# A seven-product FFN pair accumulated in two PSUM banks, and gated products turned by transposing DMAs

## The chip, the cores and the metric

The kernel runs on one core of one Trainium2 chip. The metric is device time in microseconds (us) of one execution; several executions of one build are timed and their median is taken. Beside them stands one execution that was recorded by the hardware profiler, with a span (first to last instruction) and a time of its own.

The engines of the core are named as in the profile: PE is TensorE's matmul (PEld its weight load), DVE is VectorE, ACT is ScalarE, POOL is GpSimd, SP is SyncE, on whose queue this kernel puts its DMAs.

## What is computed

Two layers of an encoder trunk over 256 tokens of width 1024. Each layer is a projection, two attention-like branches, their merge, a SwiGLU feed-forward network (FFN) and an embedding step. The change lies in the FFN:

```python
gate, up = jnp.split(rms_norm(h, g_ffn_pre) @ w_ffn_in, 2, axis=-1)     # (256,1024) @ (1024, 2*2816)
h = h + rms_norm((jax.nn.silu(gate) * up) @ w_ffn_out, g_ffn_post)       # (256,2816) @ (2816,1024)
```

## The kernel before

**Split products.** Every float32 operand is kept as two parts, a rounded high part and the remainder. `split` (L112) makes them: an ACT cast gives the high part, a DVE subtraction (through `vsub`, L108) the low part. A product of two split operands is three matmuls (`mm3`, whose matmuls carry L96). A weight unit is 512 x 512; its splitting is two ACT casts and two DVE subtractions of 128 x 1024.

**The weight stream.** `Stream` loads units over SP into two `raw` buffers (or into borrowed ones, "lent" and "big", for the pairs below), splits them up to four ahead of PE, and issues the next load (L259) when a raw buffer comes free. `ws.take()` hands a unit to PE, `ws.done()` frees it and lets the next unit be split.

**The FFN.** The hidden width 2816 is eleven blocks of 256. For each block the gate and up columns are multiplied with the normed activations of the two token halves (`hf` 0 and 1); silu(gate) times up is the *gated product* of 128 tokens x 256 hidden channels per half. To be multiplied by `w_ffn_out` it has to be turned, so that hidden channels lie on partitions, and split; `hid` holds the turned parts.

- Blocks 0 and 1 come first, each half by itself (silu on L1257), then *plain* blocks 4, 5 and 10 (`block`, silu on L1274): one unit serves both halves with 24 matmuls.
- Blocks 2-3, 6-7 and 8-9 are three *pairs* (`pair`, `seven`). The four 128x512 results of a pair (gate and up of two halves) are a 2x2 block product, and they are formed from seven unit products instead of eight, at the price of sums of activations (`sums`, once per layer) and sums of weight units (`Stream.step`: four DVE sums of 128x2048 per pair, L289 to L300). A product (`times`, matmuls on L568 or, with the plain activations, also L568) is 12 matmuls.
- In `seven`, before the change, five of the seven products went to PSUM banks of their own or were added to; three were copied out by ACT (L612, L617, L624), and five DVE sums of 128x512 put them together: `vsub(v, o, p1)`, three additions through `add` (L607), and `vsub(v, p5, c22)` ahead of the second half's silu (L1297).

**Turning.** There are two ways in the kernel. `transpose_in` (L427) and the copy of it in `block` (L1282) use PE: transposes against an identity into a PSUM bank, then `split` reads PSUM. All gated products were turned so. `Split.turn_words` is used elsewhere, for the branch outputs ("gg") and for half of the merge: ACT copies the 32-bit words apart into their two 16-bit halves (L404), a transposing DMA on SP's queue turns them (L410), ACT copies the halves together again (L414), and `split` reads SBUF.

**The order of the work.** A string fixes the order of the FFN for PE; `u` is half a plain block (one unit), a digit is a product of a pair, `o` is one unit of `w_ffn_out` for both halves (`out_step`), `p` loads what the later stages need:

```python
FFN = "uu12u34u5u67" "uo12o34o5o67" "poo12o345o67"
PLAIN, PAIRS = (4, 5, 10), (2, 6, 8)
```

Delayed work is a `Task`, a generator that yields the number of *ticks* to wait; `tick()` is called after every six matmuls or so on PE, and a task that is due puts its instructions at that place of the program. PE's turning waited 4 ticks (`WAIT_FFN`) after a block, 9 (`WAIT_PAIR`) after a pair, 3 and 4 (`WAIT_LAST`) after the last pair. `turn_words` waits 3 ticks (`SENT`) between the first ACT copy and the DMA, and 9 (`LANDED`) between the DMA and the second copy. A consumer that comes sooner forces the task (`need`). A scheduler then orders each engine's instructions by priority and modelled readiness; each engine executes its own list in order. `tc.high_priority(n)` moves instructions forward in it.

**Buffers.** PSUM has eight banks (`acc`, `aux`). The 512-wide SBUF tiles `t512` (names `t_...` in the profile) have seven buffers; a turning by words takes three of them beside the gated product.

Of the kernel before, what the change touches and what calls it, by code (L numbers as in the profile page):

```python
# [15 lines left out]
ALU = mybir.AluOpType  # L16
# [10 lines left out]

WAIT, WAIT_FIRST, WAIT_NEXT, WAIT_H, WAIT_FFN, WAIT_MIX = 6, 4, 9, 5, 4, 3
W = dict(r=5, z=6, s0=4, s=3, s1=9, o0=1, o=1, k=4, q=3, a0=1, a1=4, a2=4, a3=1, g=6)
# [11 lines left out]

WAIT_PAIR, WAIT_LAST = 9, (3, 4)
SENT, LANDED, NEXT = 3, 9, 2
# [7 lines left out]
def trunk_kernel(ctx: ExitStack, tc: tile.TileContext, a: dict, out: bass.AP):  # L51
# [158 lines left out]
    class Stream:  # L210
# [74 lines left out]
        def step(self, n, x, y, z, q):  # L285
            c = slice(0, 2048)
            if n == 1:
                self.made(x)
                nc.vector.tensor_tensor(out=x.raw[:, c], in0=x.raw[:, c], in1=z.raw[:, c], op=ALU.add)  # L289
            elif n == 2:  # L290
                self.made(y)
                nc.vector.tensor_tensor(out=z.raw[:, c], in0=z.raw[:, c], in1=y.raw[:, c], op=ALU.add)
            elif n == 3:
                self.made(x)
                nc.vector.tensor_tensor(out=x.raw[:, c], in0=x.raw[:, c], in1=y.raw[:, c], op=ALU.add)
            elif n == 4:
                self.made(z)
            elif n == 5:
                self.made(x)
                nc.vector.tensor_tensor(out=x.raw[:, c], in0=x.raw[:, c], in1=q.raw[:, c], op=ALU.add)  # L300
            elif n == 6:
                self.made(q)
            else:
                self.load()
                self.made(x)
                self.held -= 1
                self.lend = True
# [55 lines left out]
    class Split:  # L363
# [29 lines left out]

        def turn_words(self, src, k, n, hf):

            x = lambda: t512()[:, : n * P]
            w = x()
            w16 = w.bitcast(U16)
            nc.scalar.copy(  # L404
                w16.rearrange("p (s c) -> p s c", s=2), src.bitcast(U16).rearrange("p (c s) -> p s c", s=2)
            )
            yield SENT
            r = x()
            r16 = r.bitcast(U16)
            nc.sync.dma_start_transpose(out=r16.rearrange("p (r t) -> p r t", t=P), in_=w16)  # L410
            yield LANDED
            z = x()
            z16 = z.bitcast(U16)
            nc.scalar.copy(z16.rearrange("p (c s) -> p s c", s=2), r16.rearrange("p (s c) -> p s c", s=2))  # L414
            self.put(z, k, n, hf * P, P)

# [158 lines left out]
    def sums(x):  # L575
# [7 lines left out]
        def make():  # L583
# [16 lines left out]
    def seven(sp, forms, gated):  # L600
# [4 lines left out]

        def add(out, x, y):
            nc.vector.tensor_tensor(out=out, in0=x, in1=y, op=ALU.add)  # L607
# [4 lines left out]
        nc.scalar.copy(p1, c11)  # L612
# [24 lines left out]
        times(p5, quad(1, 1), False)  # L637
        vsub(v, p5, c22)
        gated(1, v, c22)
        yield  # L640
# [164 lines left out]
    for l in range(DEPTH):  # L805
# [457 lines left out]
        def block(b):  # L1263
            sg = t512()
            o = [acc(), acc()]
            for kh in range(2):
# [4 lines left out]
                if kh == 1:  # L1271
# [4 lines left out]

                    def turn():
                        yield WAIT_FFN
                        ps = aux()
                        for k in range(2):  # L1280
                            for hf in range(2):
                                nc.tensor.transpose(  # L1282
                                    ps[:, k * T + hf * P : k * T + (hf + 1) * P],
                                    sg[:, hf * 256 + k * P : hf * 256 + (k + 1) * P], ident,
                                )
                        with tc.high_priority(AHEAD):
                            hid.put(ps, 2 * b, 2, 0, T)

                    t = Task(turn(), part[0], 2 * b // 4)
                    for hf in range(2):  # L1290
# [3 lines left out]
        def pair(b):  # L1294
            def gated(hf, gate, up):
                sg = t512()
                nc.scalar.activation(sg, gate, AF.Silu)  # L1297
# [163 lines left out]
```

## Time and profile before

| what | us |
|---|---|
| median of 3 runs | 933.05 (932.12 to 935.67) |
| the profiled execution, its own time | 931.35 |
| the span of that execution, first to last instruction | 929.6 |
| first FFN matmul to the first matmul of the embedding step, layer 0 | 256.34 to 437.87 |
| the same stage of layer 1, end | 893.82 |

The mean granted TensorE clock of the profiled execution is 0.998. PE is busy for 99% of the span, DVE for 79%, ACT for 63%. A busy time is the time in which at least one instruction is under way on the engine; matmuls overlap in the pipeline, so that what a matmul costs is read from the distance between the starts of two, not from its own duration. A wait in the profile is idle time of one engine in front of an instruction, with the instruction that ended it.

### The profile page before, as it was taken

The numbers are of one execution on the slowest core, as the hardware profiler recorded it, in microseconds if no ns is written. First come the engines' busy times: TensorE is split into PE (matmuls) and PEld (weight loads), VectorE is DVE, ScalarE is ACT, GpSimd is POOL, SyncE is SP. The second block draws the span as 40 slices with busy tenths as digits, with TensorE's granted clock in tenths as the row PEclk, the third lists the DMA queues.
The fourth block names the chain that finished last, engine by engine and source line by source line (L and its number), as shares of the span: only waits on it lengthen the run. The fifth ranks groups of instructions, "written<-read, shape, count | busy, mean of one in ns | idle before, by whom it ended". The sixth has DMA issues, their size and how long they took to land.

```text
span 929.6 us, 12279 instructions
## 1 busy us (share of the span) xinstructions
PE 916.4 (99%) x4649; PEld 777.9 (84%) x4649; DVE 732.8 (79%) x933; ACT 587.4 (63%) x952; POOL 82.3 (9%) x150
## 2 busy tenths in 40 slices
PE   8999999999999999999999999999999999999996
PEld 7998888888878888888899988888888788888886
DVE  4798977556569999998789799665666798989974
ACT  5669678735467565566766686785546656656663
POOL 3500211000000000002023001200001000000000
PEclk9999999999999999999999999999999999999999
DMA  7464457767385565537555525396662937473551
GB/s 246 155 227 135 138 180 183 243 214 208 98 270 167 187 228 210 185 142 249 195 168 182 192 81 180 103 294 200 205 218 94 309 121 271 150 264 118 182 181 45
DMA packets 100760, 172.39 MB, mean 185 GB/s; under 512 B 16023, under 2 KB 39063, under 8 KB 100702
## 3 DMA queue, kind: packets, MB, share of 16 engines
q1 hardware_dynamic: 100702, 171.62, 55.8%
q8 instruction: 36, 0.59, 0.3%
q14 instruction: 22, 0.18, 0.1%
HBM read 167.41 MB, written 1.05 MB: 181 GB/s over the span
## 4 chain that ended last, share of the span: by engine, by line
PE 81%; DVE 9%; DMA 3%; ACT 2%; issue 2%; POOL 1%; SPq 0%; POOLq 0%; ACTq 0%; DVEq 0%
PE acc_0ffnin L96 11%; PE acc_1ffnin L96 7%; PE acc_0ffnin L568 6%; PE acc_0gate L96 5%; PE acc_1gate L96 5%; PE acc_1merge L96 5%; PE acc_0merge L96 5%; DVE wl_1ffnin L108 4%; PE acc_1ffnin L568 3%; PE acc_1gqk L96 2%; PE acc_0gqk L96 2%; PE acc_1ple L96 2%; PE acc_0rq L96 2%; PE acc_0gg L96 2%; PE acc_1gg L96 2%; PE acc_0v L96 2%
## 5 line engine op out<-in xcount | busy, mean ns | idle before, releaser
L96 PE MATMUL acc_1ffnin<-wh_1ffnin,big_1ffnin 128*128 128x512 f32 x176 | 56.9, 393 | 0.0
L96 PE MATMUL acc_0ffnin<-wh_0ffnin,big_0ffnin 128*128 128x512 f32 x176 | 56.9, 392 | 0.0
L112 ACT CAST wh_1ffnin<-raw_1ffnin 128x1024 fp32r<-128x1024 f32 x38 | 38.0, 1049 | 22.5 <-PE acc_1ffnin L96 7.6
L112 ACT CAST wh_0ffnin<-raw_0ffnin 128x1024 fp32r<-128x1024 f32 x38 | 37.9, 1050 | 21.0 <-PE acc_0ffnin L96 7.7
L108 DVE TENSOR_TENSOR wl_1ffnin<-raw_1ffnin,wh_1ffnin 128x1024 fp32r<-128x1024 f32 x38 | 44.8, 1219 | 4.4 <-ACT wh_1ffnin L112 4.2
L108 DVE TENSOR_TENSOR wl_0ffnin<-raw_0ffnin,wh_0ffnin 128x1024 fp32r<-128x1024 f32 x38 | 45.3, 1232 | 3.4 <-ACT wh_0ffnin L112 3.2
L96 PEld LDWEIGHTS acc_1ffnin<-wh_1ffnin,big_1ffnin 128*128 128x128 f32 x176 | 33.0, 188 | 7.0 <-ACT big_1ffnin L112 0.4
L96 PEld LDWEIGHTS acc_0ffnin<-wh_0ffnin,big_0ffnin 128*128 128x128 f32 x176 | 33.0, 188 | 6.7
L108 DVE TENSOR_TENSOR wl_1ffnin<-lent_1ffnin,wh_1ffnin 128x1024 fp32r<-128x1024 f32 x30 | 35.4, 1218 | 2.0 <-ACT wh_1ffnin L112 1.9
L108 DVE TENSOR_TENSOR wl_0ffnin<-lent_0ffnin,wh_0ffnin 128x1024 fp32r<-128x1024 f32 x30 | 35.5, 1219 | 1.8 <-ACT wh_0ffnin L112 1.7
L112 ACT CAST wh_1ffnin<-lent_1ffnin 128x1024 fp32r<-128x1024 f32 x30 | 30.2, 1050 | 8.6 <-ACT wh_1ffnin L112 3.0
L112 ACT CAST wh_0ffnin<-lent_0ffnin 128x1024 fp32r<-128x1024 f32 x30 | 30.2, 1050 | 8.6 <-PE acc_0ffnin L96 3.7
L96 PE MATMUL acc_1ffnin<-wl_1ffnin,big_1ffnin 128*128 128x512 f32 x88 | 34.3, 390 | 0.0
L96 PE MATMUL acc_0ffnin<-wl_0ffnin,big_0ffnin 128*128 128x512 f32 x88 | 34.3, 389 | 0.0
L96 PE MATMUL acc_0ffnin<-wh_0ffnin,big_0wout 128*128 128x512 f32 x96 | 31.2, 395 | 0.0
L96 PE MATMUL acc_1ffnin<-wh_1ffnin,big_1wout 128*128 128x512 f32 x96 | 31.2, 394 | 0.0
L568 PE MATMUL acc_0ffnin<-wh_0ffnin,mid_0ffnin 128*128 128x512 f32 x96 | 31.0, 390 | 0.0
L568 PE MATMUL acc_1ffnin<-wh_1ffnin,mid_1ffnin 128*128 128x512 f32 x96 | 31.0, 390 | 0.0
L108 DVE TENSOR_TENSOR wl_0gate<-raw_0gate,wh_0gate 128x1024 fp32r<-128x1024 f32 x14 | 16.5, 1221 | 15.2 <-ACT wh_0gate L112 15.2
L108 DVE TENSOR_TENSOR wl_1gate<-raw_1gate,wh_1gate 128x1024 fp32r<-128x1024 f32 x14 | 16.5, 1222 | 15.2 <-ACT wh_1gate L112 15.2
L96 PE MATMUL acc_0rq<-wh_start,big_start 128*128 128x384 f32 (+1 forms) x96 | 24.8, 343 | 1.0 <-ACT big_start L122 1.0
L96 PE MATMUL acc_1gate<-wh_1gate,big_0ple 128*128 128x512 f32 x80 | 24.8, 389 | 0.0
(655 smaller groups left out, 2948.9 us busy)
## 6 DMA issues: line engine op xcount, KB each, us to landing
raw_0ffnin<-in_w_ffn_out_dram SPq DMA_DIRECT2D x11, 1024.0 KB, 5.7
raw_1ffnin<-in_w_ffn_out_dram SPq DMA_DIRECT2D x11, 1024.0 KB, 5.0
lent_0ffnin<-in_w_ffn_in_dram SPq DMA_DIRECT2D x6, 1024.0 KB, 7.4
lent_1ffnin<-in_w_ffn_in_dram SPq DMA_DIRECT2D x6, 1024.0 KB, 7.5
raw_0rq<-in_w_in_dram SPq DMA_DIRECT2D x4, 1024.0 KB, 5.1
raw_0v<-in_w_in_dram SPq DMA_DIRECT2D x4, 1024.0 KB, 5.1
raw_0gg<-in_w_in_dram SPq DMA_DIRECT2D x4, 1024.0 KB, 5.1
raw_0gate<-in_w_o_gla_dram SPq DMA_DIRECT2D x4, 1024.0 KB, 5.1
```

What stands on the lines that cost most here:

```text
L96: return nc.tensor.matmul(o, lhsT, rhs, start=start, stop=stop)
L108: nc.vector.tensor_tensor(out=out, in0=in0, in1=in1, op=ALU.subtract)
L112: nc.scalar.copy(hi, src)
L568: nc.tensor.matmul(o, x, y, start=first and k + n == 0, stop=k == 3 and n == 2, skip_group_check=not first)
```

## The change

1. `seven` uses two PSUM banks, `a` and `v`, for products 1 to 5 and 7, and a third, `c`, for product 6. Products 3, 5 and 7 are added into `a` on top of the first, product 4 into `v` on top of the second (the matmuls run with `start` off, once what is in the bank has been read). ACT still copies out three times. Of the DVE sums, three are left: `vsub(u, v, u)`, `vsub(p5, p5, a)` and an addition `p1 = c + p1`, the last two with raised priority. The first half's silu reads SBUF (`p1`) and the second half's reads PSUM (`a`).
2. `sums` forms its sums with other signs and another order of the four; their number stays. `Stream.step` sums the weight units in another order (x+z, x+y, z+y, x+q) and makes them in the order x, x, x, y, z, q, x, where it was x, y, x, z, x, q, x.
3. All gated products but the last pair's go through `turn_words`. Per layer these are four of 128x256 (blocks 0 and 1), three of 128x512 that hold both halves of a plain block, and four of 128x512 (two pairs): 11 transposing DMAs. The last pair keeps `transpose_in` and its 3 and 4 ticks.
4. `turn_words` gets a form for both halves at once, whose second ACT copy is two copies of half the size.

```diff
         def step(self, n, x, y, z, q):
...
+            if n == 7:
+                self.load()
+            self.made((x, x, x, y, z, q, x)[n - 1])
             if n == 1:
-                self.made(x)
-                nc.vector.tensor_tensor(out=x.raw[:, c], in0=x.raw[:, c], in1=z.raw[:, c], op=ALU.add)
+                add(x, z)
             elif n == 2:
-                self.made(y)
-                nc.vector.tensor_tensor(out=z.raw[:, c], in0=z.raw[:, c], in1=y.raw[:, c], op=ALU.add)
-            elif n == 3:
-                self.made(x)
-                nc.vector.tensor_tensor(out=x.raw[:, c], in0=x.raw[:, c], in1=y.raw[:, c], op=ALU.add)
+                add(x, y)
             elif n == 4:
-                self.made(z)
+                add(z, y)
             elif n == 5:
-                self.made(x)
-                nc.vector.tensor_tensor(out=x.raw[:, c], in0=x.raw[:, c], in1=q.raw[:, c], op=ALU.add)
-            elif n == 6:
-                self.made(q)
...
+                add(x, q)
...
-        def turn_words(self, src, k, n, hf):
+        def turn_words(self, src, k, n, hf=None):
-            x = lambda: t512()[:, : n * P]
+            x = lambda: t512()[:, : n * P * (2 if hf is None else 1)]
...
-            nc.scalar.copy(z16.rearrange("p (c s) -> p s c", s=2), r16.rearrange("p (s c) -> p s c", s=2))
-            self.put(z, k, n, hf * P, P)
+            if hf is None:
+                for i in range(2):
+                    nc.scalar.copy(
+                        z16.rearrange("p (k h t s) -> p h s k t", k=2, h=2, s=2)[:, i],
+                        r16.rearrange("p (s h k t) -> p h s k t", h=2, k=2, s=2)[:, i],
+                    )
+                self.put(z, k, n, 0, T)
+            else:
+                nc.scalar.copy(z16.rearrange("p (c s) -> p s c", s=2), r16.rearrange("p (s c) -> p s c", s=2))
+                self.put(z, k, n, hf * P, P)
...
         def make():
             yield 1
             (a11, a12), (a21, a22) = x
             s2 = t512()
             vsub(a22, a21, a22)
-            vsub(s2, a11, a22)
-            vsub(a12, a12, s2)
+            vsub(s2, a22, a11)
+            nc.vector.tensor_tensor(out=a12, in0=a12, in1=s2, op=ALU.add)
             yield 1
-            vsub(a21, a21, a11)
-            for s in (a12, a22, a21, s2):
+            vsub(a21, a11, a21)
+            for s in (a22, s2, a12, a21):
...
-        (p1, v), (p3, p7) = (halves(mid()) for _ in range(2))
-        c11 = acc()
-        times(c11, quad(0, 0))
-        nc.scalar.copy(p1, c11)
+        (p1, p5), u = halves(mid()), mid()[:, 0:512]
+        a, v = acc(), acc()
+        times(a, quad(0, 0))
+        nc.scalar.copy(p1, a)
         yield
         task.need()
-        o = acc()
-        times(o, form(0))
-        nc.scalar.copy(p3, o)
+        times(v, form(0))
+        nc.scalar.copy(p5, v)
         yield
-        p5 = acc()
-        times(p5, form(1))
+        times(a, form(1), False)
+        nc.scalar.copy(u, a)
         yield
-        o = acc()
-        times(o, form(2))
-        nc.scalar.copy(p7, o)
+        times(v, form(2), False)
+        vsub(u, v, u)
         yield
-        o = acc()
-        times(o, form(3))
-        vsub(v, o, p1)
-        add(v, p5, v)
-        c12, c22 = p3, p7
-        add(c12, v, p3)
-        add(c22, v, p7)
+        times(a, form(3), False)
+        with tc.high_priority(EMPTY):
+            vsub(p5, p5, a)
         yield
-        times(c11, quad(0, 1), False)
-        gated(0, c11, c12)
+        c = acc()
+        times(c, quad(0, 1))
+        with tc.high_priority(EMPTY):
+            nc.vector.tensor_tensor(out=p1, in0=c, in1=p1, op=ALU.add)
+            gated(0, p1, u)
         yield
-        times(p5, quad(1, 1), False)
-        vsub(v, p5, c22)
-        gated(1, v, c22)
+        times(a, quad(1, 1), False)
+        gated(1, a, p5)
         yield
...
-        def turned(src, k, n, hf, wait=WAIT_FFN):
+        def turned(src, k, n, hf, wait=None):
             def turn():
-                yield wait
-                transpose_in(hid, src, k, n, hf)
+                if wait in WAIT_LAST:
+                    yield wait
+                    transpose_in(hid, src, k, n, hf)
+                else:
+                    yield from hid.turn_words(src, k, n, hf)
...
-                    def turn():
-                        yield WAIT_FFN
-                        ps = aux()
-                        for k in range(2):
-                            for hf in range(2):
-                                nc.tensor.transpose(
...
-                    t = Task(turn(), part[0], 2 * b // 4)
+                    t = Task(hid.turn_words(sg, 2 * b, 2), part[0], 2 * b // 4)
...
-                turned(sg, 2 * b, 4, hf, WAIT_LAST[hf] if b == PAIRS[-1] else WAIT_PAIR)
+                turned(sg, 2 * b, 4, hf, WAIT_LAST[hf] if b == PAIRS[-1] else None)
```

More of the change, by code (lines that the diff above doesn't have):

```diff
@@ L26 @@
 AHEAD, EMPTY, EMPTY_FIRST = 400, 100, 1600
-WAIT, WAIT_FIRST, WAIT_NEXT, WAIT_H, WAIT_FFN, WAIT_MIX = 6, 4, 9, 5, 4, 3
+WAIT, WAIT_FIRST, WAIT_NEXT, WAIT_H, WAIT_MIX = 6, 4, 9, 5, 3
 W = dict(r=5, z=6, s0=4, s=3, s1=9, o0=1, o=1, k=4, q=3, a0=1, a1=4, a2=4, a3=1, g=6)
@@ L40 @@
 OUT = (0, 1, 2, 3, 4, 5, 10, 6, 7, 8, 9)
-WAIT_PAIR, WAIT_LAST = 9, (3, 4)
+WAIT_LAST = (3, 4)
 SENT, LANDED, NEXT = 3, 9, 2
@@ L285, in step, with add @@
         def step(self, n, x, y, z, q):
-            c = slice(0, 2048)
+            def add(to, other):
+                c = slice(0, 2048)
+                nc.vector.tensor_tensor(out=to.raw[:, c], in0=to.raw[:, c], in1=other.raw[:, c], op=ALU.add)
+            if n == 7:
+                self.load()
+            self.made((x, x, x, y, z, q, x)[n - 1])
             if n == 1:
-                self.made(x)
-                nc.vector.tensor_tensor(out=x.raw[:, c], in0=x.raw[:, c], in1=z.raw[:, c], op=ALU.add)
+                add(x, z)
             elif n == 2:
-                self.made(y)
-                nc.vector.tensor_tensor(out=z.raw[:, c], in0=z.raw[:, c], in1=y.raw[:, c], op=ALU.add)
-            elif n == 3:
-                self.made(x)
-                nc.vector.tensor_tensor(out=x.raw[:, c], in0=x.raw[:, c], in1=y.raw[:, c], op=ALU.add)
+                add(x, y)
             elif n == 4:
-                self.made(z)
+                add(z, y)
             elif n == 5:
-                self.made(x)
-                nc.vector.tensor_tensor(out=x.raw[:, c], in0=x.raw[:, c], in1=q.raw[:, c], op=ALU.add)
-            elif n == 6:
-                self.made(q)
-            else:
-                self.load()
-                self.made(x)
+                add(x, q)
+            elif n == 7:
                 self.held -= 1
@@ L1275, in block @@
                         vmul(sg[:, c], o[hf][:, 256:512], sg[:, c])
-                    def turn():
-                        yield WAIT_FFN
-                        ps = aux()
-                        for k in range(2):
-                            for hf in range(2):
[L1282 to L1287, printed above, removed]
-                    t = Task(turn(), part[0], 2 * b // 4)
+                    t = Task(hid.turn_words(sg, 2 * b, 2), part[0], 2 * b // 4)
                     for hf in range(2):
```

2 lines of the change are left out of this document (removed).

## Prediction

> **What bounds the kernel now.** I read the page first: busy times, then the chain of work that ended last.
>
> ```profile
> span 929.6 us, 12279 instructions
> PE 916.4 (99%) x4649; PEld 777.9 (84%) x4649; DVE 732.8 (79%) x933; ACT 587.4 (63%) x952; POOL 82.3 (9%) x150
> PE 81%; DVE 9%; DMA 3%; ACT 2%; issue 2%; POOL 1%; SPq 0%; POOLq 0%; ACTq 0%; DVEq 0%
> ```
>
> PE holds 81% of the chain, DVE 9%. The share of the whole span hides the stages, so the windows over layer 0's FFN came next (columns: window, its length, then busy us and count of PE, PEld, DVE, ACT, POOL, clock, DMA share, GB/s):
>
> ```profile
> 266.00:300.00 34.00, 33.66 (x155) 27.27 (x155) 29.06 (x36) 22.04 (x34) 0.00 (x0) 1.00 0.64 211
> 300.00:340.00 40.00, 39.92 (x181) 32.78 (x180) 37.15 (x36) 22.89 (x30) 0.00 (x0) 1.00 0.72 260
> 340.00:390.00 50.00, 50.00 (x228) 41.31 (x227) 45.85 (x42) 29.68 (x35) 0.95 (x1) 1.00 0.51 184
> 390.00:437.80 47.80, 47.80 (x224) 39.61 (x223) 43.68 (x43) 31.29 (x40) 5.65 (x12) 1.00 0.51 178
> ```
>
> PE idles 0.42 us in 171.8 (the four lengths less the four busy times), so each instruction taken out of PE's stream should shorten the stage. But DVE is busy for 93% of 300 to 340, 92% of 340 to 390 and 91% from 390 on. It follows close behind, and ACT, at 105.9 us of 171.8 (62%), feeds it. The question is whether DVE and ACT can follow a faster PE.
>
> **PE: the transposes that go.** The turnings of layer 0, by line, and one group of four in the timeline:
>
> ```profile
> L1282 PE MATMUL aux_0ffnin<-ident,t_0ffnin x12: 270/272/329, 298.3 to 343.9; 128*128 128x128 f32 x12
> L427 PE MATMUL aux_0ffnin<-ident,t_0ffnin x32: 270/272/275, 269.8 to 425.6; 128*128 128x128 f32 x32
> ```
>
> ```profile
> 338.82 0.39 PE L96 MATMUL acc_0ffnin<-wh_0ffnin,big_0ffnin 128*128 128x512 f32 x1
> 339.05 0.60 PE L427 MATMUL aux_0ffnin<-ident,t_0ffnin 128*128 128x128 f32 x4
> 339.40 0.47 PE L96 MATMUL acc_0ffnin<-wh_0ffnin,big_0ffnin 128*128 128x512 f32 x1
> 339.72 0.39 PE L96 MATMUL acc_0ffnin<-wl_0ffnin,big_0ffnin 128*128 128x512 f32 x1
> ```
>
> The duration of 272 ns is latency; the cost is the shift of the starts. From 338.82 the second matmul after the group starts 0.90 later; two matmul steps take 0.46 (two steps of 0.23, as from 338.82 to 339.05). So four transposes cost 0.44, one 0.11. Of 44 per layer the last pair keeps 8; 36 go: 36 x 0.11 = 4.0 us per layer, **8.0 us in both**. PE's other work stays: seven products, as before.
>
> **DVE: the sums that go.** The rows of the additions in `seven`:
>
> ```profile
> L607 DVE TENSOR_TENSOR mid_0ffnin<-mid_0ffnin,mid_0ffnin x6: 681/688/693, 326.6 to 415.3; 128x512 f32<-128x512 f32 x6
> L607 DVE TENSOR_TENSOR mid_0ffnin<-acc_0ffnin,mid_0ffnin x3: 683/685/692, 325.9 to 413.9; 128x512 f32<-128x512 f32 x3
> ```
>
> Two sums less per pair, three pairs: 6 x 0.69 = 4.1 us of DVE per layer. With PE idle 0.42 us, I count no gain on the path; they buy slack, and only from the end of the first pair on (325.9). The splits of the turned parts stay, from SBUF in place of PSUM; the weight sums stay four of 128x2048. `sums` keeps four sums.
>
> **ACT, SP and DMA: what is added.** Turning by words can be priced where the kernel does it already (the "gg" tiles: the two ACT copies, the cast, the DMA's issue):
>
> ```profile
> L404 ACT COPY t_0gg<-mid_0gg x4: 1034/1042/1058, 142.0 to 156.2; 128x1024 uint16<-128x1024 uint16 x4
> L410 SPq DMA_TRANSPOSE t_0gg<-t_0gg x4: 1237/1294/5613, 143.1 to 158.9; - x4
> L414 ACT COPY t_0gg<-t_0gg x4: 1348/1358/1364, 159.8 to 170.1; 128x1024 uint16<-128x1024 uint16 x4
> DMA to landing us min/median/max: 3.1/5.1/7.7
> ```
>
> (The last line is from the view of L410.) A 512-wide turning adds 1.04 + 1.36 = 2.4 us of ACT, a 256-wide one half, by estimate: 7 x 2.4 + 4 x 1.2 = 21.6 us per layer. ACT goes from 105.9 to about 127.5 of 168, 76%: not a bound by its sum. The DMA waits 3 ticks and has 9 ticks to land; a tick is six matmuls, 6 x 0.23 = 1.4 us, so 12 us against a landing of at most 7.7. By the string, blocks 4, 5, 10 and pairs 2 and 6 are turned 8 ticks or more before `out_step` asks; no task is forced. What can hurt is order: ACT executes its list in order, and the first copy stands behind the DVE product it reads, the second behind the landing. The merge shows both (ACT's timeline, the bracket being the idle time):
>
> ```profile
> 210.27 1.05 ACT L404 COPY t_0merge<-big_0gate 128x1024 uint16<-128x1024 uint16 x1 [2.80 <-DVE big_0gate L1213]
> 215.38 1.35 ACT L414 COPY t_0merge<-t_0merge 128x1024 uint16<-128x1024 uint16 x1 [1.22 <-DMA t_0merge<-t_0merge]
> ```
>
> Queued behind such a copy are the casts of the next weight units; DVE waits for these, then PE. The tight place is the first pair, where DVE and PE run side by side:
>
> ```profile
> 276.76 1.22 DVE L108 TENSOR_TENSOR wl_0ffnin<-raw_0wout,wh_0ffnin 128x1024 fp32r<-128x1024 f32 x1 [4.26 <-ACT wh_0ffnin L112]
> 287.91 2.28 DVE L289 TENSOR_TENSOR lent_0ffnin<-lent_0ffnin,lent_0ffnin 128x2048 f32<-128x2048 f32 x1
> 295.52 2.35 DVE L108 TENSOR_TENSOR wl_0ffnin<-raw_0ffnin,wh_0ffnin 128x1024 fp32r<-128x1024 f32 x2
> 298.45 2.35 DVE L108 TENSOR_TENSOR wl_0ffnin<-lent_0ffnin,wh_0ffnin 128x1024 fp32r<-128x1024 f32 x2
> 295.57 2.01 ACT L112 CAST wh_0ffnin<-lent_0ffnin 128x1024 fp32r<-128x1024 f32 x2 [0.48 <-ACT t_0ffnin L1274]
> 298.66 0.39 PE L96 MATMUL acc_0ffnin<-wl_0ffnin,big_0wout 128*128 128x512 f32 x1
> ```
>
> The unit subtracted at 295.52 has its first half by 296.7, and PE reads it at 298.66: slack 2.0 us. PE comes there earlier by the three groups of two taken out since DVE began this stretch at 276.76 (half of 0.44 each, 0.66). Also, step 2 now uses the sum x+z itself, so sum (287.91), cast (1.0) and subtraction stand in a row; DVE has other small work for that wait, so I charge 0.3 to it and leave 1.0 us of slack. Blocks 4 and 5 each put a copy of 1.04 among the casts, possibly after a wait like the 2.80. ACT's lead over DVE is 1.9 (first half cast by 296.6, used at 298.45). So one such copy holds DVE for up to 2.80 + 1.04 - 1.9 = 1.9 us and PE for 0.9; a copy that does not wait holds PE for nothing. Between 0 and 1.9 a layer (one or both blocks) I take 0.75, towards the waiting end because DVE is saturated: **+1.5** in all. On SP a transposing DMA takes 1.24 to 5.6 us of the queue, ahead of weight loads; the loads' own waits for buffers (below) hide the usual 1.3:
>
> ```profile
> SPq L259 <- DVE wl_0ffnin L108: 90.4, 17, 15.3
> ```
>
> Here SP waits 90 us of the stage; with that cover gone, a load would be late by 1.3 and so would its cast.
>
> **New waits in `seven`.** Half 0 of the last pair still has only 3 ticks to its transposes, and a DVE sum now precedes its silu:
>
> ```profile
> 416.88 0.60 ACT L1297 ACTIVATE t_0ffnin<-acc_0ffnin 128x512 f32<-128x512 f32 x1 [1.08 <-PE acc_0ffnin L568]
> 418.15 0.68 DVE L105 TENSOR_TENSOR t_0ffnin<-mid_0ffnin,t_0ffnin 128x512 f32<-128x512 f32 x1
> 420.76 0.60 PE L427 MATMUL aux_0ffnin<-ident,t_0ffnin 128*128 128x128 f32 x4
> ```
>
> The product is there at 418.83, 1.9 us early. The sum takes 0.69 and can wait for one DVE subtraction (1.2), one cast (1.0) and another subtraction: late by 0 to 2.2 us; with raised priority nearer the low end, 0.3 a layer: **+0.6**. The second half loses a sum from its chain, a gain only in slack. The reuse of the banks: product 3 goes onto the bank that product 1 left, once ACT has copied it.
>
> ```profile
> 297.48 0.57 ACT L612 COPY mid_0ffnin<-acc_0ffnin 128x512 f32<-128x512 f32 x1
> 304.40 5.44 PE acc_0ffnin L568 x24
> ```
>
> That copy ended at 298.05, product 3 began at 304.40: free. In the third pair ("345") product 5 follows product 3 with only product 4 (12 x 0.23 = 2.7 us) between, and a copy behind a pair of casts takes 2.0 + 0.57: 0 to 1 us, I take 0.2 a layer, **+0.4**. The Trainium skill (Perfetto Trace Analysis, Matmuls) says that matmul groups should rotate through different PSUM banks so that the emptying of one overlaps the next. The 6.3 us between these two rows let the kernel break that rule; without such cover the sum would lose a copy of 0.57 per reuse.
>
> **Sum.** -8.0 + 1.5 + 0.6 + 0.4 = -5.5 us. The profiled execution, 931.35 (span 929.6 and 1.75 around it), would be 925.9; it stands 1.7 under the median of 933.05, so the predicted median is **927.5**.
>
> **Rivals.** *All hidden.* The three charges vanish: 8.0 us, 925.0. For it: gg and merge turn by words with PE hardly idle. Against: DVE has room there, not here.
>
> *DVE sets the pace of the first pair.* Its sums go only after 325.9, so the PE groups removed between 276 and 321 (three of two, two of four, 1.54 a layer) bring nothing, and the row sum-cast-subtraction adds a whole 1.05: 4.0 - 1.54 - 1.05 = 1.4 a layer, 2.8 in all, **930.2**. For it: the DVE share of 93% in the windows. Against: the 2.0 us of slack. The Trainium skill (Perfetto Trace Analysis, Identifying the Most-Contended Engine) judges PE by LDWEIGHTS time, not matmul time; by it DVE (45.85 of 50) leads PEld (41.31), and the trace agrees about the shares, not about PE's idle time.
>
> *ACT is held, and it gets slower.* If each of the 22 turnings holds ACT as the merge's did, 2.80 less ACT's lead of 1.9 reaches DVE: 22 x 0.9 = 20 us, of which PE's slack takes 2.0 a layer: 16 - 8 = 8 us slower, **941**. From 0.55 us per turning on it takes the whole gain, from 0.76 it makes the kernel slower by over 0.5%. For it: in-order ACT. Against: outside the first pair DVE idles for 8% (340 to 390) and catches up, and the scheduler can put casts that are ready ahead of a copy that is not. The Trainium skill (VectorE: DVE Perf Modes, Rules for kernel authors) says to transpose 128x128 on TensorE if a PSUM destination is acceptable; these rows agree about the cost of each: 0.44 us of PE against 2.4 of ACT and 1.3 of SP.
>
> **Numbers.** Chances: the forecast with its bounds 0.45 (faster by over 0.5% in 0.36 of it), all hidden 0.18, DVE's pace 0.23, ACT held 0.14. A measurement of this kernel can tell about 0.5%, 4.7 us, from no change: faster 0.36 + 0.18 = 0.54, same 0.09 + 0.23 = 0.32, slower 0.14. Range: from all hidden with the 0.42 us of PE's idle time per layer (924.2) to 935, which takes in 930.2 and a forecast whose charges triple (2.5 x 3 = 7.5, 932.6) and leaves out most of ACT held.
>
> **What would show it.** Right: 36 fewer transposes a layer, ffnin stages shorter by 2 to 4 us each, PE idle under 2 us in each, DVE about 4 us less busy, ACT about 22 more. DVE's pace: PE idle on weight remainders in the first pair. ACT held: ACT idle at L404 or L414 of several us, casts late, PE idle all through the stage. The forecast is wrong if PE idles more than 4 us per FFN, or if transposing DMAs land after their 12 us.

## The result, and the profile after

The kernel after takes 943.68 us (median of 4 runs, 940.99 to 947.02) against 932.59 for the kernel before beside it: ratio 1.0115, 95% interval 1.0074 to 1.0157, slower by 11.1 us. One execution of e3 below (1090.22 us, granted clock 0.784) ran in a slower state of the chip and is left out; all others had a clock of 0.989 or more. The profiled execution took 942.78 (before: 931.35). From the page of after, the span, the busy times and the chain of waits:

```profile
span 941.1 us, 12200 instructions
PE 913.1 (97%) x4577; PEld 771.3 (82%) x4577; DVE 725.4 (77%) x921; ACT 624.5 (66%) x1002; POOL 81.1 (9%) x150
PE 48%; DVE 9%; DMA 6%; ACT 4%; issue 3%; POOL 1%; SPq 0%; POOLq 0%; ACTq 0%; DVEq 0%
```

PE has 72 instructions less, DVE 7.4 us less and ACT 37 us more (forecast: 72, 8.2 and 43). PE's share of the chain, 48% after 81%, can't be compared: the shares of this chain add up to 71% of the span, those of the one before to 98%. What PE waits for is read from the stages. The windows over layer 0's FFN, as before the change (the last one ends at the stage's new end):

```profile
266.00:300.00 34.00, 33.41 (x147) 26.60 (x147) 28.28 (x35) 25.24 (x40) 0.00 (x0) 1.00 0.65 199
300.00:340.00 40.00, 40.00 (x178) 33.03 (x177) 37.63 (x35) 28.48 (x36) 0.00 (x0) 1.00 0.77 255
340.00:390.00 50.00, 48.05 (x208) 38.45 (x207) 42.80 (x40) 36.97 (x46) 0.95 (x1) 1.00 0.69 227
390.00:446.50 56.50, 48.96 (x222) 39.89 (x221) 47.59 (x48) 36.64 (x49) 7.54 (x14) 0.95 0.58 197
```

The first pair (to 340) is as full as before. PE idles 1.95 us in the third window and 7.5 in the last. In PE's timeline these are the waits of over 0.5 us from the second pair on (the bracket is the idle time and what ended it), first layer 0, then layer 1:

```profile
346.06 0.50 PE L96 MATMUL acc_0ffnin<-wl_0ffnin,big_0ffnin 128*128 128x512 f32 x1 [0.71 <-DVE wl_0ffnin L108]
358.47 0.50 PE L96 MATMUL acc_0ffnin<-wl_0ffnin,big_0ffnin 128*128 128x512 f32 x1 [0.52 <-DVE wl_0ffnin L108]
367.94 0.50 PE L96 MATMUL acc_0ffnin<-wl_0ffnin,big_0ffnin 128*128 128x512 f32 x1 [0.68 <-DVE wl_0ffnin L108]
444.71 1.97 PE L431 MATMUL aux_0ffnout<-ident,h 128*128 128x128 f32 x8 [7.54 <-DVE h L529]
...
810.94 0.50 PE L96 MATMUL acc_1ffnin<-wl_1ffnin,big_1ffnin 128*128 128x512 f32 x1 [2.10 <-DVE wl_1ffnin L108]
824.37 0.50 PE L96 MATMUL acc_1ffnin<-wl_1ffnin,big_1ffnin 128*128 128x512 f32 x1 [1.61 <-DVE wl_1ffnin L108]
833.84 0.50 PE L96 MATMUL acc_1ffnin<-wl_1ffnin,big_1ffnin 128*128 128x512 f32 x1 [0.74 <-DVE wl_1ffnin L108]
862.58 0.50 PE L96 MATMUL acc_1ffnin<-wl_1ffnin,big_1ffnin 128*128 128x512 f32 x1 [0.55 <-DVE wl_1ffnin L108]
```

There are two kinds: one wait of 7.5 us at the end of layer 0's FFN, which layer 1 doesn't have, and short waits for weight remainders from the second pair on, in both layers.

**The long wait.** The last turning of layer 0's FFN reads `h`, which needs the reciprocal norm (rstd) that POOL makes. POOL's timeline, first before, then after:

```profile
428.49 0.85 POOL L688 TENSOR_TENSOR t_0ffnin<-mid_0ffnin 128x256 f32<-128x256 f32 x1 [46.82 <-DMA mid_0ffnin<-in_g_q_norm_dram]
...
433.36 0.30 POOL L477 TENSOR_SCALAR rstd_0ffnout<-ss_0ffnout 128x1 f32<-128x1 f32 x1
```

```profile
437.85 1.10 POOL L685 TENSOR_TENSOR t_0ffnin<-mid_0ffnin 128x256 f32<-128x256 f32 x1 [54.90 <-DMA mid_0ffnin<-in_g_q_norm_dram]
...
441.68 1.14 POOL L689 TENSOR_TENSOR t_0ffnin<-mid_0ffnin 128x64 f32<-128x64 f32 x4
442.92 0.30 POOL L481 TENSOR_SCALAR rstd_0ffnout<-ss_0ffnout 128x1 f32<-128x1 f32 x1
```

POOL executes in order, and ahead of the rstd stand the products of layer 1's rope tables, which wait for a gain's load. Both starts are 9.4 to 9.6 us later. SP's timeline says why, before and then after:

```profile
421.59 0.42 SPq L682 DMA_DIRECT2D mid_0ffnin<-in_rope_cos_dram  x1
...
422.58 0.46 SPq L330 DMA_DIRECT2D mid_0ffnin<-in_g_q_norm_dram  x1
...
426.98 3.85 SPq L259 DMA_DIRECT2D raw_0ffnin<-in_w_ple_gate_dram  x2
```

```profile
426.41 4.76 SPq L259 DMA_DIRECT2D raw_0ffnin<-in_w_ple_gate_dram  x2
431.28 1.22 SPq L679 DMA_DIRECT2D mid_0ffnin<-in_rope_cos_dram  x1
432.56 0.46 SPq L680 DMA_DIRECT2D mid_0ffnin<-in_rope_sin_dram  x1
433.06 0.46 SPq L326 DMA_DIRECT2D mid_0ffnin<-in_g_q_norm_dram  x1
```

The tables' loads changed places in SP's list with two weight loads that wait for buffers, though the change touches neither. Layer 1 has no tables to prepare, so no such wait. The Trainium skill (Perfetto Trace Analysis, Tensor Engine Instruction) says that ACT, DVE and GpSimd are strict FIFOs; these rows agree.

**The short waits.** They are waits for remainders, which DVE makes. DVE's timeline of after in layer 1's second pair, ahead of the remainders that PE gets at 810.94, 824.37 and 833.84:

```profile
806.19 2.29 DVE L288 TENSOR_TENSOR lent_1ffnin<-lent_1ffnin,big_1ffnin 128x2048 f32<-128x2048 f32 x1
808.40 0.68 DVE L108 TENSOR_TENSOR big_1ffnin<-t_1ffnin,big_1ffnin 128x512 fp32r<-128x512 f32 x1
809.00 0.75 DVE L105 TENSOR_TENSOR t_1ffnin<-acc_1ffnin,t_1ffnin 128x256 f32<-128x256 f32 x2
809.67 2.35 DVE L108 TENSOR_TENSOR wl_1ffnin<-raw_1ffnin,wh_1ffnin 128x1024 fp32r<-128x1024 f32 x2
...
820.29 2.29 DVE L288 TENSOR_TENSOR lent_1ffnin<-lent_1ffnin,raw_1ffnin 128x2048 f32<-128x2048 f32 x1 [0.97 <-DMA raw_1ffnin<-in_w_ffn_in_dram]
...
831.96 0.69 DVE L108 TENSOR_TENSOR mid_1ffnin<-mid_1ffnin,acc_1ffnin 128x512 f32<-128x512 f32 x1 [3.64 <-PE acc_1ffnin L572]
832.57 4.62 DVE L108 TENSOR_TENSOR wl_1ffnin<-raw_1ffnin,wh_1ffnin 128x1024 fp32r<-128x1024 f32 x4
```

and ACT's in the same pair:

```profile
800.59 1.05 ACT L112 CAST wh_1ffnin<-lent_1ffnin 128x1024 fp32r<-128x1024 f32 x1 [3.35 <-DVE lent_1ffnin L288]
...
804.87 1.41 ACT L412 COPY t_1ffnin<-t_1ffnin 128x512 uint16<-128x512 uint16 x2
...
807.20 1.99 ACT L112 CAST wh_1ffnin<-raw_1ffnin 128x1024 fp32r<-128x1024 f32 x2
```

Each of the three waits has something else last in front of it.

- The cast at 807.20 is of the unit whose remainder PE gets at 810.94, 2.1 us late. Four copies of turnings (L400, L412) stand ahead of it in ACT's list, and from 800.6 on ACT has no gap until the loads run out at 824. But the first half of that cast is done by 808.3, and the subtraction starts at 809.67: DVE has no gap (of over 0.15 us) from 795.8 to 814.3, and a weight sum, the split of a turned product and two gated products stand ahead.
- Before 824.37 (1.61 us late) the weight sum at 820.29 waits 0.97 for a weight load. SP issued it at 813.39, behind a transposing DMA that went out at 812.05, once the first ACT copy of block 10's turning (810.98 to 812.03) was there. Counted from the FFN's first matmul that load goes out at 92.1 us in after and at 92.9 in e4 below, but at 88.2 in e6, which leaves out these DMAs, and at 88.0 in e7, which leaves out the copies.
- Before 833.84 (0.74 us late) no copy stands in the way: DVE stands 3.64 us at `vsub(p5, p5, a)`, which the change gave a raised priority, until product 5 is there, and the next unit's subtractions are queued behind it. Layer 0 has the same 3.64 us before its wait at 367.94.

DVE's 77% and ACT's 66% of the span say nothing of this stretch.

### The profile page after: what moved, and what is told of

Read it like the earlier page. It is cut to its first block, busy times and chain, and to the rows that moved or that the text cites. A ratio compares the mean times of both kernels' runs of the same rounds, so it can differ in the third digit from the quotient of the medians.

```text
span 941.1 us, 12200 instructions
## 1 busy us (share of the span) xinstructions
PE 913.1 (97%) x4577; PEld 771.3 (82%) x4577; DVE 725.4 (77%) x921; ACT 624.5 (66%) x1002; POOL 81.1 (9%) x150
## 4 chain that ended last, share of the span: by engine, by line
PE 48%; DVE 9%; DMA 6%; ACT 4%; issue 3%; POOL 1%; SPq 0%; POOLq 0%; ACTq 0%; DVEq 0%
PE acc_0ffnin L96 7%; PE acc_1ffnin L96 6%; PE acc_1gate L96 5%; PE acc_1merge L96 5%; DVE wl_1ffnin L108 4%; PE acc_0ffnin L572 4%; PE acc_1gqk L96 2%; PE acc_1ple L96 2%; PE acc_1gg L96 2%; PE acc_1v L96 2%; PE acc_1ffnin L572 2%; DMA lent_0ffnin<-in_w_ffn_in_dram 1%; PE acc_1rq L96 1%; PE aux_1gla L96 1%; DVE wl_0ffnin L108 1%
## 5 line engine op out<-in xcount | busy, mean ns | idle before, releaser
L112 ACT CAST wh_0ffnin<-lent_0ffnin 128x1024 fp32r<-128x1024 f32 x30 | 30.3, 1053 | 11.1 <-DVE lent_0ffnin L288 7.4
```

Source lines behind the costliest of these rows:

```text
L112: nc.scalar.copy(hi, src)
```

## The experiments

Each was timed in five rounds beside the kernel before. Stages are counted from the first starts in the tile views: *FFN* from the first matmul of `acc_0ffnin` (or `acc_1ffnin`) to the first of the embedding step (in before 256.34 to 437.71 and 712.25 to 893.66), *between* from there to layer 1's FFN (one profiled execution each).

| run | median us | ratio to before, 95% | FFN 0 | between | FFN 1 |
|---|---|---|---|---|---|
| before | 932.3 | | 181.4 | 274.5 | 181.4 |
| after | 943.68 | 1.0115 (1.0074 to 1.0157) | 189.8 | 275.0 | 183.8 |
| e1 seven alone | 944.93 | 1.0139 (1.0125 to 1.0152) | 192.2 | 276.0 | 182.8 |
| e2 turning alone | 928.69 | 0.9961 (0.9949 to 0.9973) | 180.3 | 274.4 | 179.7 |
| e3 after, tables early | 939.93 | 1.0076 (1.0061 to 1.0091) | 186.0 | 275.6 | 183.3 |
| e4 after, tables late | 934.32 | 1.0023 (1.0012 to 1.0034) | 181.5 | 276.5 | 183.2 |
| e5 seven, tables late | 938.63 | 1.0066 (1.0047 to 1.0085) | 183.3 | 277.0 | 182.0 |
| e6 e4 without DMAs | 932.21 | 1.0002 (0.9987 to 1.0018) | 179.4 | 276.4 | 180.1 |
| e7 e4 without copies | 928.19 | 0.9955 (0.9936 to 0.9974) | 177.9 | 276.7 | 177.9 |
| e8 e4, sum deferred | 935.89 | 1.0044 (1.0027 to 1.0061) | 183.5 | 278.6 | 181.8 |
| e9 before, gates first | 941.88 | 1.0110 (1.0094 to 1.0126) | 190.7 | 276.2 | 181.5 |
| e10 unit order alone | 950.45 | 1.0200 (1.0185 to 1.0216) | 200.2 | 275.4 | 183.2 |
| e11 e4, 12 on PE | 931.75 | 0.9996 (0.9986 to 1.0006) | 180.5 | 277.1 | 180.0 |
| e12 e2, block 5 on PE | 927.80 | 0.9961 (0.9947 to 0.9975) | 180.4 | 274.3 | 179.3 |

**e1 and e2, the two halves of the change.** e1 takes `step`, `sums` and `seven` of after and leaves the turnings on PE; e2 takes the turnings and leaves those three as before.

> The kernel before with the two-bank seven, its sums and its order of the weight units; every turning stays on PE. Theory (two causes: rope tables queued behind the w_ple_gate loads hold POOL's rstd at the end of layer 0's FFN, about +8.9 us; turnings that crowd ACT and SP around the second pair, about +7 us; against them 8.0 us of transposes gone): in this kernel's program order on SP the tables stand behind both w_ple_gate loads, as in the kernel after, so the 7 to 8 us idle time of PE before layer 0's last turning is here too, and nothing else changes: 932.6 + 8.9 = 941.5, between 938 and 943. Rival 1 (the turnings alone cost the time, the seven products are free or gain a little): 930 to 933. Rival 2 (the new order of the weight sums starves PE in the second pair of both layers): PE idles before VectorE's weight remainders at about the second pair in both layers, and the time is 944 or more.

> The kernel after with the seven products, sums and weight order of the kernel before; the turnings go by DMA. Its program order on SP has the rope tables ahead of the w_ple_gate loads, as before. Theory: no idle time of several us at the end of layer 0's FFN; the 8.0 us of transposes are gained and most of it is lost again around the second pair, where ACT's copies and SP's transposing DMAs delay casts and weight loads: about 932.6 - 8 + 7 = 931.6, between 928 and 934. Rival 1 (turnings alone cost it): 943. Rival 2 (the weight order starves PE): the gain of 8.0 shows, 924 to 926.

The turnings alone make the kernel 3.6 us faster; the seven alone makes it 12.6 slower, more than the whole change. The long wait is in e1, and not in e2. PE's timeline of e1, its two largest waits:

```profile
301.21 0.50 PE L564 MATMUL acc_0ffnin<-wh_0ffnin,mid_0ffnin 128*128 128x512 f32 x1 [1.62 <-ACT wh_0ffnin L112]
...
447.91 0.69 PE L423 MATMUL aux_0ffnout<-ident,h 128*128 128x128 f32 x2 [7.30 <-DVE h L521]
```

Rival 1 (the turnings alone cost the time) is gone. Rival 2 has its time (944 or more) and not its sign: no wait of the second pair is in e1. e1 was 3.4 over its number and 1.9 over its bounds: it has waits of its own, as the one at 301.21 (1.62 in each layer), where ACT's copying out of product 2 waits for PE and holds the next cast, and behind the long wait PE runs 5.0 us at a clock of 0.50 (last section). e2 is inside its bounds for a wrong reason: the second pair, where its expectation put the loss, has no wait over 0.4 us there; the largest is at the end of the first pair (0.94 us at 319.36). So the waits of the second pair need both halves of the change.

**e3 and e4, the tables elsewhere.**

```diff
-            ropes = rope_tables(l + 1)
+            with tc.high_priority(100):              # e3
+                ropes = rope_tables(l + 1)
...
         embedded.need()
+        if l + 1 < DEPTH:                            # e4, in place of the call above
+            ropes = rope_tables(l + 1)
```

> The kernel after, with layer 1's rope tables issued with a raised priority, so that SP has them ahead of the second w_ple_gate load. Theory: POOL's products of the tables are done before the rstd of layer 0's FFN output is asked for, PE's 7.7 us wait there goes: 943.7 - 8.9 = 934.8, between 933 and 937. Rivals 1 and 2 (the tables are a side show and PE waits there for something else that comes last next): 941 to 944, with PE's wait before layer 0's last turning still over 4 us and another releaser in its bracket.

> The kernel after, with the rope tables' loads and products put behind the whole FFN of layer 0, so that POOL does both rstd first. Theory: as with the early tables, the wait of PE at the end of layer 0's FFN goes (933 to 937), unless the tables come too late for layer 1's first rope, which would show as a wait of VectorE for POOL in layer 1's first stage. If SP's order (the loads) and not POOL's order made the loss, this one doesn't mend it: 941 to 944.

e3 missed its bounds and gained only 3.8 of 8.9: the priority moved the tables past one of the two gate loads, and the wait shrank to half, with the same releaser. In e4 POOL makes the first rstd at 430.99, PE doesn't wait there at all, and 9.4 us of the 11.1 are gone (the stage between the FFNs, where the tables' loads and products now fall, grew by 1.5 to 2 us). PE's timeline of e3:

```profile
441.78 0.44 PE L431 MATMUL aux_0ffnout<-ident,h 128*128 128x128 f32 x2 [3.56 <-DVE h L529]
```

**e9, the order of the loads put into the kernel before.** The call moves a few lines down, and the tables are tied behind the stream's last load:

```diff
+            with tc.issue_after(line["load"].ins):
+                ropes = rope_tables(l + 1)
```

> The kernel before, with one thing changed: layer 1's rope tables are loaded behind the first two w_ple_gate loads on SP, as in the kernel after; POOL's list stays (table products, then both rstd). Theory (this order alone makes the wait at the end of layer 0's FFN): the gate loads go out until about 431, the gains land and POOL starts about 437.5, its products take 5 us, rstd, h and PE's last turning follow: PE waits 7 to 8 us before the last turning, 932 + 8 = 940, between 938 and 942. Rival (it takes a faster PE or the turnings for it): 932 to 934.

It costs 9.6 us by itself, with the same row:

```profile
446.17 0.69 PE L427 MATMUL aux_0ffnout<-ident,h 128*128 128x128 f32 x2 [7.36 <-DVE h L525]
```

So neither the turnings nor the banks are needed for the long wait. That is more than the idle time of 7.4; the last section shows what the clock adds.

**e10, what moved the loads.** The kernel before with after's `step` and the products in its order; copies, sums and banks are those of before.

```diff
-            for s in (a12, a22, a21, s2):
+            for s in (a22, s2, a12, a21):
...
+        p5 = acc()
+        times(p5, form(0))
+        yield
         o = acc()
-        times(o, form(0))
-        nc.scalar.copy(p3, o)
+        times(o, form(1))
+        vsub(v, o, p1)
+        add(v, p5, v)
```

> The kernel before with the change's order of the weight units and products (b11, x+z, x+z+y, b22, z+y, q, x) and nothing else of it: five sums, banks as before, turnings on PE. In its program order the rope tables stand behind three w_ple_gate loads, one more than after. Theory (the order of the units is what moves the tables; two banks and three sums have no part in it): PE waits at the end of layer 0's FFN, and longer than after, because the third gate load went out 4 us behind the second: 11 to 14 us, 932 + 12 = 944, between 941 and 948, with the 1.8 us wait for ACT's cast of the second unit in the first pairs too. Rival (it is the two banks): no wait there, 930 to 935.

PE's longest wait there, and SP's list:

```profile
456.45 0.69 PE L423 MATMUL aux_0ffnout<-ident,h 128*128 128x128 f32 x2 [12.06 <-DVE h L521]
```

```profile
433.53 4.33 SPq L259 DMA_DIRECT2D raw_0ffnin<-in_w_ple_gate_dram  x2
...
442.50 0.37 SPq L259 DMA_DIRECT2D raw_0ffnout<-in_w_ple_gate_dram  x1
442.92 0.50 SPq L678 DMA_DIRECT2D mid_0ffnin<-in_rope_cos_dram  x1
```

Three gate loads ahead, 12.1 us of wait. So `step` and the order of the products are enough to move the tables: in before, e2 and e12 the tables stand ahead of the gate loads, in after, e1 and e10 behind two or three. Why the scheduler ranks them so was not looked into. At 950.45 e10 is 2.5 over its bounds: besides the long wait it has one of 1.96 for a cast in layer 0's second pair, behind which the clock was at 0.50 for 3.4 us, and in its first pairs PE waits 1.64 and 1.72 for a gated product, not for the forecast cast.

**e6, e7 and e8, the short waits.** All three start from e4. e6 takes the DMA out of the FFN's turnings, e7 the two copies; e8 holds the sum z+y back in DVE's list. The edits, in that order:

```diff
-            r = x()
-            r16 = r.bitcast(U16)
-            nc.sync.dma_start_transpose(out=r16.rearrange("p (r t) -> p r t", t=P), in_=w16)
+            r16 = w16                                  # in the FFN
...
+            if "ffnin" in part[0]:
+                yield SENT
+                z = x()
+                nc.sync.dma_start_transpose(out=z.bitcast(U16).rearrange("p (r t) -> p r t", t=P), in_=src.bitcast(U16))
+                yield LANDED
+                self.put(src, k, n, 0 if hf is None else hf * P, T if hf is None else P)
+                return
...
             elif n == 4:
-                add(z, y)
+                with tc.issue_after(self.last.ins):    # the split of product 4's unit
+                    add(z, y)
```

> The kernel of e4 with the transposing DMAs of the FFN left out: the second ACT copy reads the first one's result, so the products are regrouped but not turned. ACT's copies, their order and PE's work stay. PE idles about 3 us in the second pair of layer 0 of e4 and 5 us in that of layer 1. If SP's transposing DMAs (three in 10.7 us there) and their traffic, which hold weight loads, are the cause: 927 to 929. If ACT's copies or VectorE's order of the weight sums are the cause: 933 to 935, with the same waits for weight remainders at the same places.

> The kernel of e4 with both ACT copies of each FFN turning left out: the DMA transposes the product as it is, and the splits read the product unturned, so the transposing DMAs run but their result isn't used. If ACT's copies among the casts are the cause of PE's waits in the second pairs: 926 to 929. If SP's transposing DMAs are: 933 to 935. If VectorE's order of the weight sums is the cause: 932 to 935.

> The kernel of e4 with the third weight sum of each pair (z+y, 2.29 us of VectorE) held until the split of the unit of product 4 is done; in e4 it stands two units earlier, ahead of the split of the w_ffn_out unit that PE waits for in layer 1. If this place in VectorE's in-order list is the cause: the waits of 2.4 us go and the time is 929 to 931. If ACT's copies or SP's transposing DMAs make VectorE late: 933 to 936, the same waits, or a new one before product 5.

Without the copies 6.1 us come back (0.68% by the ratios), inside e7's bounds for the copies. Without the DMAs it is 2.1 (0.21%): e6 lies between its two forecasts, and its interval overlaps e4's. The windows from 785 to 825 (layer 1's second pair) of e4, e6 and e7, in that order:

```profile
785.00:825.00 40.00, 37.43 (x156) 29.72 (x155) 33.14 (x31) 28.56 (x37) 0.00 (x0) 0.96 0.76 218
```

```profile
785.00:825.00 40.00, 38.55 (x167) 30.65 (x166) 34.49 (x32) 30.78 (x38) 0.00 (x0) 1.00 0.44 155
```

```profile
785.00:825.00 40.00, 39.84 (x176) 32.66 (x175) 37.61 (x34) 25.36 (x32) 0.00 (x0) 1.00 0.71 233
```

In e7 PE is busy for 39.84 of 40 us with the transposing DMAs still on SP, and both FFNs take 177.9: 3.5 us less than before, so the transposes' gain of 4.0 a layer is real. In e6 the first wait of the second pair goes too (2.15 us in e4's layer 1, 0.21 in e6); the later ones stay, with the same 3.64 us of DVE at `vsub(p5, p5, a)` ahead of the last. The stages overstate it: 1.7 of e4's 183.2 us in layer 1 are a fall of the clock behind that wait (last section). By the totals the copies are the larger cause, the DMAs a smaller one. How they act is only in part shown: copies, DVE's list and SP's queue hold each other, as the rows of after show (the DMAs at least through SP's queue; traffic isn't told apart), and e6 and e7 also leave out one and two of the three `t512` tiles of a turning. e8 missed: in layer 1 the wait of 2.15 became 1.19 and the stage 1.4 us shorter, but layer 0's became 2.0 longer, and the total didn't fall. The place of that sum is a part of layer 1's wait at most.

**e5, e11 and e12.** e5 is e1 with e4's tables. e11 is e4 with block 10 and the first pair turned on PE; e12 is e2 with block 5 turned on PE.

```diff
-                turned(sg, 2 * b, 4, hf, WAIT_LAST[hf] if b == PAIRS[-1] else None)
+                turned(sg, 2 * b, 4, hf, WAIT_LAST[hf] if b == PAIRS[-1] else 9 if b == PAIRS[0] else None)   # e11
...
-                    t = Task(hid.turn_words(sg, 2 * b, 2), part[0], 2 * b // 4)
+                    t = Task(turn() if b == PLAIN[-1] else hid.turn_words(sg, 2 * b, 2), part[0], 2 * b // 4)  # e11; e12: PLAIN[1]
```

(`turn` is the block's turning on PE as before; in e11 `turned` uses `transpose_in` for any wait that is not None.)

> The kernel of e1 (two-bank seven, turnings on PE) with the rope tables put behind the FFN as in e4. Theory (the seven's new unit order lets SP put the tables behind the w_ple_gate loads; that is nearly all that it costs): 944.9 less PE's 7.5 us and the 0.7 after it = 936.7, between 935 and 938; what is left over the kernel before (4 us) is the 1.8 us wait for ACT's cast of the second unit in the first pair of each layer. Rival (the seven costs time at many places): over 939.

> The kernel of e4 with the turnings of block 10 and of the first pair (two halves) back on PE, 12 of 36 transposes a layer: their ACT copies and DMAs fell into the second pair, where e4 loses 3 and 5 us. Theory (ACT's copies among the casts there, and in a smaller part the DMAs, make VectorE's remainders late): the waits go, 12 x 0.11 x 2 = 2.6 us come back on PE: 934.3 - 8 + 2.6 = 929, between 928 and 931. Rival (the copies of the other turnings, or the pair's own new unit order, make them late): 934 to 937.

> The kernel of e2 (turnings by DMA, the seven as before) with block 5's turning back on PE: its first ACT copy stands ahead of the casts of four unit halves (e2, layer 0: copy at 315.6, casts from 316.6), and PE waits 1.6 us for them in each layer. Theory: that wait goes, 4 transposes a layer (0.44) come back: 928.7 - 2 x 1.2 = 926.4, between 925.5 and 927.5. Rival (the casts are late because PE's product and VectorE's product come late, not because of the copy): 928.5 to 930.

e5, at 938.63, is 0.6 over its bounds: even with the tables cured, the seven alone is slower by 6.7, of which the two waits of 1.62 and the longer stage between the FFNs (2.5) make most. e11 removed the waits for weight remainders in the second pair, and at 931.75 it is between theory and rival, 0.75 above the theory's bound: PE's turning of the pair now waits once a layer for DVE's split of an earlier turning (1.07 and 0.81 us). e12, at 927.80, can't be told from e2, and its mechanism missed: the wait for the remainder stayed at 1.01 us (0.94 in e2) though no copy stood ahead of the cast. Nor were the casts late (314.90 to 316.9), so that its rival holds only in this, that a product comes late: DVE stands 1.88 us at `v = o - p1` until product 5 is there, and the subtractions of the next unit are queued behind it:

```profile
317.34 0.69 DVE L108 TENSOR_TENSOR mid_0ffnin<-acc_0ffnin,mid_0ffnin 128x512 f32<-128x512 f32 x1 [1.88 <-PE acc_0ffnin L576]
317.95 2.35 DVE L108 TENSOR_TENSOR wl_0ffnin<-raw_0ffnin,wh_0ffnin 128x1024 fp32r<-128x1024 f32 x2
```

e2 and e12 beat both kernels (0.9961 each, not to be told apart): the version to keep is the turning without the new seven.

## Why the prediction was wrong

The forecast was 927.5 (924.2 to 935.0); it measured 943.68, outside the range and on the other side. The prediction's own sign of being wrong, over 4 us of idle PE in an FFN, came twice: 10.6 us in layer 0 and 5.6 in layer 1.

- **"8.0 us in both" for the transposes: right.** 36 fewer a layer, and where the cover holds (e7) each FFN is 3.5 us shorter, with 1.1 and 1.5 us of PE's waits left.
- **DVE's sums, "no gain on the path": held, as far as shown.** With the new order and PE's turnings in both, layer 1's FFN takes 183.2 us with five sums (e10) and 182.8 with three and two banks (e1), one execution each.
- **The step that failed first: the new order of the weight units.** The prediction took `Stream.step` as four sums of 128x2048 as before and 0.3 us of a chain in the first pair. It followed what the new order does to the products, and not what it does to the lists of SP and POOL behind them. Its remark that "the loads' own waits for buffers (below) hide the usual 1.3" looked at what stands in front of a weight load; what stood behind one was layer 1's tables, then POOL's products, then the rstd, then `h`, then PE. e9 puts this one exchange at 9.6 us, of the change's 11.1, and undoing it (e4) gives 9.4 back.
- **The charge of 1.5 for ACT's copies: right in kind, wrong in place and size.** It stood at the first pair, where after loses nothing (PE 40.00 of 40.00). The copies collide one pair later, where the turnings of the first pair and of block 10 fall together with casts chained to sums: "outside the first pair DVE idles for 8% ... and catches up" failed. The copies of all turnings cost 6.1 us (e4 against e7), the DMAs about 2.1 (e4 against e6). A part of this pair's loss belongs to no charge: the 3.64 us in which DVE stands at `vsub(p5, p5, a)`, ahead of waits of 0.68 and 0.74.
- **A landing within the 12 us of nine ticks: right.** Landing took 2.4 to 8.6 us (the bound taken was 7.7), and no second copy in the FFN waited for it.
- **The two charges in `seven` (0.6 and 0.4):** neither wait is among those of the new profile; the last pair shows at most 0.29 us before its transposes.
- **Rivals.** *ACT held* gave 941, near the result, but by 22 turnings that each hold ACT; three first copies a layer waited, 3.8 us in layer 0. The copies cost 6.1 us where it had 16, in the second pair, and the larger part of the time came from the tables. *All hidden* and *DVE's pace* fell, with the first pair unharmed; one pair later DVE is indeed the engine without a gap (795.8 to 814.3).

The Trainium skill (VectorE: DVE Perf Modes, Rules for kernel authors) says to transpose 128x128 on TensorE where a PSUM destination is acceptable. By these runs it depends on the rest of the list: with the old seven the DMA way gains 3.6 us (e2), with the new one putting 12 of 36 transposes back on PE gains 2.6 (e11 against e4).

## What to carry to other kernels

When a change reorders the issue of loads, follow each queue that they share to the end of the stage and past it: what stands behind a load that waits for a buffer (here tables, then an in-order POOL, then a norm) pays for all of it. A gain on the full engine is only kept if the engines that feed it have room in the very stretch where the new work falls, not on average. Time the halves of a two-part change apart: here one half gains 3.6 us and the other loses 12.6.

## What the hardware showed beside that

A long idle time of PE costs more than itself. PE's windows in after (length, busy, granted clock), around the wait of 7.5 us:

```profile
437.00:444.70 7.70, 0.17 (x1) 0.74 0.97 329
444.70:446.20 1.50, 1.49 (x7) 0.50 0.79 317
446.20:448.00 1.80, 1.80 (x8) 0.62 0.03 14
448.00:450.00 2.00, 2.00 (x11) 1.00 0.00 0
```

For 3.3 us after the wait PE runs at 0.50 to 0.62 of its clock, a loss of about 1.4 us by estimate (1.5 x 0.50 + 1.8 x 0.38). In e9 it is more. PE is back at 446.17, and the window from there is

```profile
446.17:451.49 5.32, 5.32 (x17) 0.50 0.22 89
```

which is 2.7 us by the same estimate. With the wait of 7.4 and another of 1.03 at 328.58 that makes 11.1; this execution took 943.16, 10.9 over the median of before.

A short wait can cost the clock too. e4 around its wait of 2.15 us (ended at 805.34), then after around its 2.10 us (ended at 810.94):

```profile
803.20:806.60 3.40, 1.26 (x5) 1.00 0.00 0
806.60:810.01 3.41, 3.41 (x9) 0.50 0.89 65
```

```profile
805.98:809.39 3.41, 2.86 (x13) 1.00 0.41 77
809.39:812.80 3.41, 1.86 (x8) 1.00 0.01 2
812.80:816.20 3.40, 3.40 (x16) 1.00 1.09 95
```

In e4 the clock was at 0.50 for 3.41 us, a loss of 1.7 by estimate; in after it stayed at 1.00. Behind waits of PE the clock's times at 0.50 last 3.41 us or a multiple of it (6.83, 10.24, 13.65) in all these traces. Cut each span into stretches of 3.41 us, counted from its changes of clock: e4's wait lies in one stretch, after's is parted over two, with 0.55 and 1.55 us. In all the traces no stretch at full clock with 1.55 us of idle PE or less is followed by one at 0.50, every one with 1.96 us or more is, and of five with 1.56 to 1.72 one is (e8). The Trainium skill (TensorE: Matmul & The Clock Gate, What's actually happening) says that the clock is halved after an idle window of about 3.4 us and restored after a busy one. The wait of 7.5 us agrees; e4's shows that the window need not be idle throughout, and the measurement decides.
